# A decoder layer on one core: gate matrices from float32r parts, and differential heads with tokens on partitions

## The chip, the cores and the metric

The kernel runs on one core of a Trainium2 chip. The metric is the device time of one execution in microseconds, as the median over runs. The core has five engines with instruction streams of their own: TensorE (matrix products; PE in the profile, its weight loads PEld), VectorE (DVE), ScalarE (ACT), GpSimd (POOL) and SyncE (SP, which here issues most transfers). Products are accumulated in PSUM, eight banks of 128 partitions x 512 f32; everything else on the chip lies in SBUF.

## The reference, cut to what matters

256 tokens of width 2048 pass one layer. Two token mixers run side by side (latent attention, and differential attention with 8 heads), their gated sum is projected and added to the residual; then comes an expert retrieval over 128 x 128 experts.

A differential head takes the difference of two causal softmaxes, multiplies it with v, and normalizes each token's 128 outputs:

```
p = _causal_probs(q1b, k1, blk, scale) - lam * _causal_probs(q2b, k2, blk, scale)
o = einsum('bhqk,bkhd->bqhd', p, v)
o = rmsnorm(o, g_subln) * (1.0 - lambda_init)
```

The expert retrieval gives each token 8 heads x 16 choices; a choice is a pair (row, col) of keys with a gate, and the expert's number is row * 128 + col:

```
a = gelu(einsum('chkd,cd->chk', expert_u[ec], hc))
w = gc * a
out = einsum('chk,chkd->cd', w, expert_v[ec])
```

## The kernel before, in words

Most weight products are made with float32r operands, a 32-bit type: a weight tile is split into a part `hi` rounded to float32r (ScalarE, L79) and the rest `lo` (VectorE, L84), and both are multiplied (L143 to L145, L161 to L163, L1019). Products on plain f32 operands stand where no split is made, the columns of the expert keys (L721) among them.

**Order of the work.** The program is written in one stream. Helpers with `yield` (a head, a norm) are jobs that `advance` moves on by one part at every eighth product of a block (`tick`), three jobs at a time, so that their short instructions fall between the products. The framework then plans the order of the instructions on each engine from modelled durations and from when tiles and banks come free; each engine works through its own list in that order and waits where something is not ready. `issue_after(x)` keeps an instruction behind x on its own engine. A tile has a tag and a number of buffers; a new tile with that tag waits for the readers of the one that it replaces. PSUM banks are handed out in the same way: `bank(tag)` has one buffer a tag (b0, b1, b2, t, m, n), `ps_s` two (s). `ps_m` is the bank m.

**Differential heads** (L558 to L580). They run as jobs beside the gate projections (L587 to L592). A head makes scores and probabilities (L564, `probs`), transposes the probabilities (L493), copies them (L496), and multiplies with v in `pv` (L503, L504), with v as the stationary operand: the result has the 128 channels on partitions and the 256 tokens along the free axis. ScalarE copies it out of bank m (L573). The sum of squares over channels is then a sum over partitions: ScalarE squares (L205), TensorE multiplies the squares with a column of ones (L216, two products of one column), VectorE scales (L222), GpSimd takes the power -1/2 (L225). The factor of a token must come to all partitions, which two products with the identity do (L231), and VectorE multiplies (L579). `split_scaled` writes both parts for the next projection (L192, L193).

**Expert retrieval.** For 192 of the tokens all experts are worked out densely. 128 columns c of keys follow each other; a column is 16 products of 192 tokens (L721) accumulated in one of four banks (b1, m, n, b0 in turn), and ScalarE writes their Gelu into B, a tile [row, c, token] (L907). The other 64 tokens fetch their own experts by gathers: GpSimd issues them (L862) and VectorE works on the rows (L875, L880). B must be multiplied with each token's gate matrix G[row, col], the sum of gates at that pair. G of a token is the product of two one-hot tiles over its 128 choices: R[choice, row] (GpSimd, L927) and C[choice, col], which carries the gate (VectorE, L928). A step (`g_step`, L932) takes four tokens: four products into one s bank (L937), then VectorE multiplies the columns that are done into B (L947) and copies G into the columns that are not yet done (L949); those are multiplied later by GpSimd (L911) when their Gelu comes (L910). `onehots(t4 + 2)` is called at the head of step t4, with 12 buffers each for R and C. The 48 steps are spread over columns 32 to 119 by a count of products (L729). rowT, colT and gateT hold a token's rows, columns and gates with choices on partitions; `r_tr` (L824) fills them.

After the last column the products with expert_v follow (L1019), with the banks b2, t, m, n and s.

Of the kernel before, what the change touches and what calls it, by code (L numbers as in the profile page):

```python
# [7 lines left out]
F32 = mybir.dt.float32  # L8
F32R = mybir.dt.float32r
U32 = mybir.dt.uint32  # L10
AF = mybir.ActivationFunctionType
ALU = mybir.AluOpType
# [6 lines left out]
EPS = 1e-6  # L19
LAMBDA_INIT = 0.8 - 0.6  # L20
NH = 8
NB = 128
TD = 192
TG = T - TD
NLOW = 64
C0 = 32
NG4 = TD // 4
# [5 lines left out]
def hybrid_peer(tc, a, out):  # L33
    nc = tc.nc
    es = ExitStack()

    def pool(stack, name, bufs=1, side=None, space=None):
        kw = {} if space is None else dict(space=space)
        return stack.enter_context(
            tc.tile_pool(name=name, bufs=bufs, side=side, reuse_waits="tile", **kw))  # L40
# [4 lines left out]
    ident = cst.tile([128, 128], F32, name="ident")  # L45
    iota = cst.tile([128, 128], F32, name="iota")
    ones = cst.tile([128, 1], F32, name="ones")
    nhalf = cst.tile([128, 2], F32, name="nhalf")

    state = {"n": 0, "max": 3, "fill": 0, "b": 0, "g": 0, "c": 0, "f": 0, "s": 0, "w": 0}  # L50
# [120 lines left out]
    wk = pool(ups, "wk")  # L171
    pp = pool(es, "pp", space=PSUM)

    def bank(tag):
        return pp.tile([128, 512], F32, tag=tag, name=tag, bufs=1)
# [5 lines left out]
    def ps_s():  # L181
        return pp.tile([128, 512], F32, tag="s", name="s", bufs=2)

    def ps_m():
        return pp.tile([128, 512], F32, tag="m", name="m", bufs=1)

    def w1(name, tag, bufs=2):
        return wk.tile([128, T], F32, tag=tag, name=name, bufs=bufs)

    def split_scaled(dst, src, g, n=256):  # L190

        nc.scalar.activation(dst[:, 0:n], src, AF.Copy, scale=g)  # L192
        nc.vector.scalar_tensor_tensor(dst[:, n:2 * n], src, g, dst[:, 0:n].bitcast(F32),  # L193
                                       op0=ALU.mult, op1=ALU.subtract)
# [265 lines left out]
    gs = uc.tile([128, 1], F32, name="gs")  # L460
# [7 lines left out]
    def probs(scores, scale, lam=None, prev=None):  # L468

        s = wk.tile([128, 384], F32, tag="sc", name="sc", bufs=3)  # L470
        nc.vector.scalar_tensor_tensor(s, scores[:, 0:384], scale, mask, op0=ALU.mult, op1=ALU.add)
        mx = wk.tile([128, 2], F32, tag="mx", name="mx", bufs=4)
        sm = wk.tile([128, 2], F32, tag="sm", name="sm", bufs=4)
        for tb, c0, c1 in TBK:
            nc.vector.tensor_reduce(mx[:, tb:tb + 1], s[:, c0:c1], axis=AX.X, op=ALU.max, negate=True)
            nc.scalar.activation(s[:, c0:c1], s[:, c0:c1], AF.Exp, bias=mx[:, tb:tb + 1],
                                 accum_out=sm[:, tb:tb + 1])
        rc = wk.tile([128, 2], F32, tag="rc", name="rc", bufs=4)
        nc.vector.reciprocal(rc, sm)
        if lam is not None:  # L480
            nc.vector.tensor_scalar(rc, rc, lam, None, op0=ALU.mult)
        for tb, c0, c1 in TBK:
            if prev is None:
                nc.vector.tensor_scalar(s[:, c0:c1], s[:, c0:c1], rc[:, tb:tb + 1], None, op0=ALU.mult)
            else:
                nc.vector.scalar_tensor_tensor(s[:, c0:c1], s[:, c0:c1], rc[:, tb:tb + 1],
                                               prev[:, c0:c1], op0=ALU.mult, op1=ALU.add)
        return s

    def transposed(s):  # L490
        pt = bank("t")
        for j in range(3):
            nc.tensor.transpose(pt[:, j * 128:(j + 1) * 128], s[:, j * 128:(j + 1) * 128], ident)  # L493

        sT = wk.tile([128, 384], F32, tag="sT", name="sT", bufs=2)
        nc.scalar.activation(sT, pt[:, 0:384], AF.Copy)  # L496
        return sT

    def pv(sT, v, h):

        po = ps_m()
        hs = slice(h * 128, (h + 1) * 128)
        nc.tensor.matmul(po[:, 0:256], lhsT=v[:, 0, hs], rhs=sT[:, 0:256], start=True, stop=False)  # L503
        nc.tensor.matmul(po[:, 128:256], lhsT=v[:, 1, hs], rhs=sT[:, 256:384], start=False, stop=True)  # L504
        return po
# [32 lines left out]
    dv = dfp.tile([128, 2, 1024], F32, name="dv")  # L538
# [5 lines left out]
    for j in range(2):  # L544
        pss = [ps_blk(), ps_blk()]
        group(u_dv, xg, KD, pss)
        for tb in range(2):
            nc.scalar.activation(dv[:, tb, j * 512:(j + 1) * 512], pss[tb], AF.Copy,
                                 scale=r1c[:, tb:tb + 1])
# [5 lines left out]
    oTb = gtp.tile([128, NH, 512], F32R, name="oTb")  # L555
    gt = gtp.tile([128, 32, T], F32, name="gt")

    def diff_head(h):  # L558
        s = None
        for i in range(2):  # L560
            sc = ps_s()
            r0 = i * 64
            for tb, c0, c1 in TBK:
                nc.tensor.matmul(sc[:, c0:c1], lhsT=dq[r0:r0 + 64, h, tb * 128:(tb + 1) * 128],  # L564
                                 rhs=dk[r0:r0 + 64, h, 0:c1 - c0], start=True, stop=True)
            s = probs(sc, 64.0 ** -0.5) if i == 0 else probs(sc, 64.0 ** -0.5, nlam, s)
        yield
        yield
        sT = transposed(s)
        yield  # L570
        po = pv(sT, dv, h)
        on = w1("on", "on", 3)
        nc.scalar.activation(on, po[:, 0:256], AF.Copy)  # L573
        yield
        nm = Norm(1)
        nm.add(on)
        v = nm.col()
        yield
        nc.vector.tensor_mul(on, on, nm.row(v))  # L579
        split_scaled(oTb[:, h], on, gs)  # L580

    for h in range(NH):
        job(diff_head(h))
# [20 lines left out]
    for j in range(KD):  # L604
        m = []
        for u, o, b in ((u_oa, oTa, j), (u_ob, oTb, 16 + j)):
# [4 lines left out]
                                           op0=ALU.add, op1=ALU.mult)  # L611
# [9 lines left out]
    gw = pool(gws, "gw", side="right")  # L621
    rowT = gw.tile([128, 2, 128], F32, name="rowT")
    colT = gw.tile([128, 2, 128], F32, name="colT")
    gateT = gw.tile([128, 2, 128], F32, name="gateT")

    hrep = gw.tile([128, D], F32, name="hrep")
    gidx = gw.tile([128, 64], U32, name="gidx")
# [22 lines left out]
    nm = Norm(KD, nc.gpsimd)  # L650
# [101 lines left out]
    def ps_g():  # L752
        return ps_s().rearrange("p (a b) -> p a b", a=4)
# [11 lines left out]
    for tb in (1, 0):  # L765
# [58 lines left out]
        def r_tr(env=env, tb=tb):  # L824
            pg = ps_g()
            for n, key in enumerate((0, 1, "g")):
                nc.tensor.transpose(pg[:, n, :], env[key].rearrange("p h k -> p (h k)"), ident)
            for n, dst in enumerate((rowT, colT, gateT)):
                nc.vector.tensor_copy(dst[:, tb, :], pg[:, n, :])

        steps.append(r_alloc)
        steps += [lambda b=b, f=r_list: f(b) for b in range(16)]
# [16 lines left out]
        if tb == 1:  # L849
            steps.append(r_list_experts)  # L850
        steps.append(r_tr)


# [43 lines left out]
    def Bsl(c0, c1):  # L897
        if c0 >= NLOW:
            return Bhigh[0][:, c0 - NLOW:c1 - NLOW]
        return Blow[:, c0:c1]  # L900
# [17 lines left out]
    RC = {}  # L918

    def onehots(t4):  # L920
        rc = []
        for i in range(4):
            tb, tt = divmod(4 * t4 + i, 128)
            R = gp.tile([128, 128], F32, tag="R", name="R", bufs=12)
            C = gp.tile([128, 128], F32, tag="C", name="C", bufs=12)
            row, col, gate = [x[:, tb, tt:tt + 1] for x in (rowT, colT, gateT)]
            nc.gpsimd.tensor_scalar(R, iota, row, None, op0=ALU.is_equal)  # L927
            nc.vector.tensor_scalar(C, iota, col, gate, op0=ALU.is_equal, op1=ALU.mult)  # L928
            rc.append((R, C))
        RC[t4] = rc  # L930

    def g_step(t4):  # L932
        if t4 + 2 < NG4:
            onehots(t4 + 2)
        pg = ps_g()
        for i, (R, C) in enumerate(RC.pop(t4)):
            nc.tensor.matmul(pg[:, i, :], lhsT=R, rhs=C, start=True, stop=True)  # L937
        ts_ = slice(4 * t4, 4 * t4 + 4)
        n = state["c"]
        for c0, c1 in sorted({(0, min(n, NLOW)), (NLOW, max(n, NLOW)), (min(n, NLOW), NLOW),  # L940
                              (max(n, NLOW), NB)}):
            if c0 == c1:
                continue
            bv = Bsl(c0, c1)[:, :, ts_].rearrange("p c t -> p t c")
            g = pg[:, :, c0:c1]
            if c0 < n:
                nc.vector.tensor_mul(bv, bv, g)  # L947
            else:
                nc.vector.tensor_copy(bv, g)  # L949
        state["g"] += 1  # L950

    GU0, GU = 14, 80 / 128
# [17 lines left out]
    gps = ExitStack()  # L970
    gp = pool(gps, "gp")
    onehots(0)
    onehots(1)
    fill += [lambda t4=t4: g_step(t4) for t4 in range(NG4)]
    for c in range(C0, NB):
        ps = ps_u()
# [84 lines left out]
    for half in range(2):  # L1061
# [17 lines left out]
        for c in range(NB):  # L1079
            raw = fetch(a["ev"][half, c])  # L1080
            hl = split(raw)
            parts = [[p[:, q * 512:(q + 1) * 512] for p in hl] for q in range(2)]
# [144 lines left out]
```

## Time and profile before

| | us |
|---|---|
| median of 3 runs | 2114.86 (2112.35 to 2115.91) |
| the profiled execution, its own time | 2112.38 |
| its span, first to last instruction | 2110.6 |
| TensorE busy in the span | 2088.1 |
| VectorE busy | 1423.9 |
| ScalarE busy | 791.9 |
| GpSimd busy | 527.0 |

The span is the time between the first and the last instruction of the program; the execution has 1.8 us around it. A busy time is the union of an engine's instructions. The chain that ended last is followed back from the last instruction, at each step to what released it, so its pieces show what a stretch of time was spent on: where TensorE's products follow each other, a piece is what a product adds, while the duration of a single instruction also has the part in which it overlaps its neighbours.

### The profile page before, as it was taken

To read this page: it belongs to the slowest core of one execution; us is meant where nothing else is said; L and a number is where in the kernel's file an instruction comes from. 1 tells how busy PE (TensorE), PEld (TensorE's weight loads), DVE (VectorE), ACT (ScalarE), POOL (GpSimd) and SP (SyncE) were. 2 spreads that over 40 slices of the span, in tenths; PEclk is the share of its full clock that TensorE was granted. 3 is DMA by queue.
4 is the path that set the end of the run, shared out by engine and by line. 5 is a ranking of instruction groups with operands and counts; after the bars stand their busy time and mean duration, and the time that the engine had idled before them with its cause. 6 is when DMAs were issued, how large, how long until landed. Compare 5 with 4: busy or idle time off the path is not lost.

```text
span 2110.6 us, 30529 instructions
## 1 busy us (share of the span) xinstructions
PE 2088.1 (99%) x11446; PEld 1855.9 (88%) x11446; DVE 1423.9 (67%) x2507; ACT 791.9 (38%) x1310; POOL 527.0 (25%) x511
## 2 busy tenths in 40 slices
PE   9999999999999999999999999999999999999998
PEld 7887888888888899999999999999788888888775
DVE  7677667657865988444555555554788888788774
ACT  5545456555554530100000000001455555455554
POOL 0000000000023212335666667662111111112100
PEclk9999999999999999999999999999999999999999
DMA  6563643555566566898888888888888888888774
GB/s 220 180 209 109 201 158 124 190 190 190 190 204 220 166 218 245 295 344 317 316 315 313 319 316 309 310 325 301 320 324 311 322 306 318 310 320 308 300 283 144
DMA packets 132708, 546.78 MB, mean 259 GB/s; under 512 B 15120, under 2 KB 15696, under 8 KB 116048
## 3 DMA queue, kind: packets, MB, share of 16 engines
q1 hardware_dynamic: 112032, 404.60, 54.3%
q0 software_dynamic: 19520, 136.91, 17.4%
q10 hardware_dynamic: 1008, 3.32, 0.4%
q8 instruction: 90, 1.47, 0.3%
q14 instruction: 58, 0.48, 0.1%
HBM read 537.89 MB, written 4.19 MB: 257 GB/s over the span
## 4 chain that ended last, share of the span: by engine, by line
PE 96%; DMA 2%; DVE 1%; issue 0%; ACT 0%; DVEq 0%; POOLq 0%; POOL 0%; ACTq 0%; SPq 0%
PE b L143 19%; PE b L721 16%; PE b L145 10%; PE s L1019 8%; PE n L721 8%; PE m L721 8%; PE m L1019 5%; PE n L1019 5%; PE b L1019 4%; PE t L1019 4%; PE s L937 2%; DMA raw<-in_ev 2%; PE b L161 1%; PE b L163 1%; PE b L162 1%; DVE lo L84 1%
## 5 line engine op out<-in xcount | busy, mean ns | idle before, releaser
L84 DVE TENSOR_TENSOR lo<-raw,hi 128x1024 fp32r<-128x1024 f32 (+1 forms) x504 | 611.9, 1219 | 267.4 <-ACT hi L79 132.5
L79 ACT ACTIVATE hi<-raw 128x1024 fp32r<-128x1024 f32 (+1 forms) x504 | 532.2, 1057 | 527.2 <-PE b L143 131.5
L721 PE MATMUL b<-h,raw 128*128 128x192 f32 x2048 | 342.0, 326 | 0.0
L721 PEld LDWEIGHTS b<-h,raw 128*128 128x128 f32 x2048 | 333.1, 190 | 0.0
L143 PE MATMUL b<-xg,hi 128*128 128x512 f32 x912 | 323.2, 397 | 0.0
L145 PE MATMUL b<-xg,lo 128*128 128x256 f32 x912 | 256.2, 281 | 1.6 <-DVE lo L84 1.6
L143 PEld LDWEIGHTS b<-xg,hi 128*128 128x128 f32 x912 | 171.2, 188 | 42.6 <-issue 4.3
L1019 PE MATMUL s<-hi,wt 128*128 128x512 f32 x512 | 202.9, 397 | 0.0
L145 PEld LDWEIGHTS b<-xg,lo 128*128 128x128 f32 x912 | 171.7, 188 | 2.7 <-DVE lo L84 2.6
L721 PE MATMUL n<-h,raw 128*128 128x192 f32 x1024 | 173.3, 326 | 0.0
L721 PE MATMUL m<-h,raw 128*128 128x192 f32 x1024 | 173.3, 326 | 0.0
L862 POOL DMA_INDIRECT rows<-in_evn,gidx x64 | 91.6, 1430 | 310.2 <-DVE gacc L880 276.3
L721 PEld LDWEIGHTS m<-h,raw 128*128 128x128 f32 x1024 | 166.9, 190 | 0.0
L721 PEld LDWEIGHTS n<-h,raw 128*128 128x128 f32 x1024 | 166.9, 190 | 0.0
L875 DVE SCALAR_TENSOR_TENSOR rows<-rows,hrep 128x2048 f32<-128x2048 f32 x64 | 148.7, 2324 | 14.3 <-DMA rows<-in_eun,gidx 12.9
L880 DVE SCALAR_TENSOR_TENSOR gacc<-rows,gwt,gacc 128x2048 f32<-128x2048 f32 x63 | 148.3, 2354 | 1.2 <-DMA rows<-in_evn,gidx 1.2
L927 POOL TENSOR_SCALAR R<-iota,rowT 128x128 f32<-128x128 f32 x192 | 133.9, 709 | 43.1 <-PE s L937 40.5
L862 POOL DMA_INDIRECT rows<-in_eun,gidx x64 | 76.3, 1192 | 253.2 <-DVE rows L875 193.1
L911 POOL TENSOR_TENSOR Bhigh<-Bhigh,ut 128x192 f32<-128x192 f32 (+28 forms) x64 | 98.9, 1546 | 88.1 <-ACT ut L910 80.5
L1019 PEld LDWEIGHTS s<-hi,wt 128*128 128x128 f32 x512 | 96.0, 188 | 23.9 <-issue 0.5
L1019 PE MATMUL s<-lo,wt 128*128 128x512 f32 x256 | 101.4, 396 | 2.5 <-DVE lo L84 2.5
L928 DVE TENSOR_SCALAR C<-iota,colT,gateT 128x128 f32<-128x128 f32 x192 | 62.8, 379 | 60.6 <-PE s L937 60.2
(322 smaller groups left out, 3444.3 us busy)
## 6 DMA issues: line engine op xcount, KB each, us to landing
raw<-in_eu SPq DMA_DIRECT2D x256, 512.0 KB
raw<-in_ev SPq DMA_DIRECT2D x256, 512.0 KB
raw<-in_w_in SPq DMA_DIRECT2D x133, 512.0 KB
raw<-in_w_out SPq DMA_DIRECT2D x32, 512.0 KB
raw<-in_w_q SPq DMA_DIRECT2D x32, 512.0 KB
raw<-in_w_o_mla SPq DMA_DIRECT2D x16, 512.0 KB
raw<-in_w_o_diff SPq DMA_DIRECT2D x16, 512.0 KB
raw<-in_w_uq SPq DMA_DIRECT2D x9, 512.0 KB
```

The costliest lines, as they stand in the source:

```text
L79: state["hi"] = nc.scalar.activation(hi[:, c], raw[:, c], AF.Copy).ins
L84: state["lo"] = nc.vector.tensor_sub(lo[:, c], raw[:, c], hi[:, c].bitcast(F32)).ins
L143: nc.tensor.matmul(ps[0:m, 0:512], lhsT=hi, rhs=act[:, k, :], start=(k == 0), stop=False)
L145: state["mm"] = nc.tensor.matmul(ps[0:m, 0:256], lhsT=lo, rhs=act[:, k, 0:256], start=False, stop=(k == nk - 1)).ins
L721: mm = nc.tensor.matmul(ps[:, 0:TD], lhsT=u_raw[-1][:, k % 8 * 128:(k % 8 + 1) * 128], rhs=h2[:, k], start=(k == 0), stop=(k == KD - 1), s ...
L862: nc.gpsimd.indirect_dma_start(out=g, out_offset=None, in_=a["eun" if which == "u" else "evn"], in_offset=bass.IndirectOffsetOnAxis(ap=gid ...
L875: nc.vector.scalar_tensor_tensor(g, g, 1.0, hrep, op0=ALU.mult, op1=ALU.mult, accum_out=gdot[:, j:j + 1])
L880: nc.vector.scalar_tensor_tensor(gacc, g, gwt[:, j:j + 1], gacc, op0=ALU.mult, op1=ALU.add)
L911: nc.gpsimd.tensor_mul(b[:, 0:n], b[:, 0:n], t[:, 0:n])
L927: nc.gpsimd.tensor_scalar(R, iota, row, None, op0=ALU.is_equal)
L928: nc.vector.tensor_scalar(C, iota, col, gate, op0=ALU.is_equal, op1=ALU.mult)
L1019: nc.tensor.matmul(o, lhsT=l, rhs=r, start=first and i == 0, stop=last and i == len(ops) - 1, skip_group_check=True)
```

## The change

A head's product with v takes the transposed probabilities as the stationary operand, so tokens come to lie on partitions: three products of 128 columns. The sum of squares of a token is then a sum along the free axis, which ScalarE accumulates while it squares (one instruction for each half of the tokens), and the factor is a scalar of each partition, applied by VectorE straight from bank m. Two transposes into bank n bring the result back to channels on partitions, and `split_scaled` reads them from there.

The gate of a token is kept as a rounded float32r part gh, its negative ng, and the rest gl. R is float32r; C has 256 columns, the one-hot with gh in the first half, made by ScalarE as Relu(gh - gh * Abs(col - iota)), and the one-hot with gl in the second, made by VectorE. One product for each token gives both halves of G. They are added as they leave the banks: ScalarE copies the second half out, VectorE adds the first where B is multiplied at once, and otherwise adds both into B. A step has two halves of two tokens, each in a bank of its own (b2 and t, or the two s). `onehots` runs one step ahead in place of two, with 8 buffers in place of 12.

```diff
--- before.py
+++ after.py
@@ -568,16 +568,32 @@
         yield
         sT = transposed(s)
         yield
-        po = pv(sT, dv, h)
+
+        po = ps_m()
+        hs = slice(h * 128, (h + 1) * 128)
+        for tb, parts in ((0, ((0, 0),)), (1, ((1, 0), (2, 1)))):
+            for i, (c, kb) in enumerate(parts):
+                nc.tensor.matmul(po[:, tb * 128:(tb + 1) * 128], lhsT=sT[:, c * 128:(c + 1) * 128],
+                                 rhs=dv[:, kb, hs], start=(i == 0), stop=(i == len(parts) - 1),
+                                 skip_group_check=True)
         on = w1("on", "on", 3)
-        nc.scalar.activation(on, po[:, 0:256], AF.Copy)
-        yield
-        nm = Norm(1)
-        nm.add(on)
-        v = nm.col()
-        yield
-        nc.vector.tensor_mul(on, on, nm.row(v))
-        split_scaled(oTb[:, h], on, gs)
+        ss = wk.tile([128, 2], F32, tag="nv", name="nv", bufs=4)
+        for tb in range(2):
+            cs = slice(tb * 128, (tb + 1) * 128)
+            nc.scalar.activation(on[:, cs], po[:, cs], AF.Square, accum_out=ss[:, tb:tb + 1])
+        nc.vector.tensor_scalar(ss, ss, 1.0 / 128, EPS, op0=ALU.mult, op1=ALU.add)
+        r = wk.tile([128, 2], F32, tag="nr", name="nr", bufs=4)
+        nc.gpsimd.tensor_tensor(r, ss, nhalf, op=ALU.pow)
+        for tb in range(2):
+            cs = slice(tb * 128, (tb + 1) * 128)
+            nc.vector.tensor_scalar(on[:, cs], po[:, cs], r[:, tb:tb + 1], None, op0=ALU.mult)
+        yield
+        yield
+        pt = bank("n")
+        for tb in range(2):
+            cs = slice(tb * 128, (tb + 1) * 128)
+            nc.tensor.transpose(pt[:, cs], on[:, cs], ident)
+        split_scaled(oTb[:, h], pt[:, 0:256], gs)
 
     for h in range(NH):
         job(diff_head(h))
@@ -621,7 +637,10 @@
     gw = pool(gws, "gw", side="right")
     rowT = gw.tile([128, 2, 128], F32, name="rowT")
     colT = gw.tile([128, 2, 128], F32, name="colT")
-    gateT = gw.tile([128, 2, 128], F32, name="gateT")
+
+    ghT = gw.tile([128, 2, 128], F32R, name="ghT")
+    ngT = gw.tile([128, 2, 128], F32, name="ngT")
+    glT = gw.tile([128, 2, 128], F32, name="glT")
 
     hrep = gw.tile([128, D], F32, name="hrep")
     gidx = gw.tile([128, 64], U32, name="gidx")
@@ -825,8 +844,11 @@
             pg = ps_g()
             for n, key in enumerate((0, 1, "g")):
                 nc.tensor.transpose(pg[:, n, :], env[key].rearrange("p h k -> p (h k)"), ident)
-            for n, dst in enumerate((rowT, colT, gateT)):
+            for n, dst in enumerate((rowT, colT)):
                 nc.vector.tensor_copy(dst[:, tb, :], pg[:, n, :])
+            nc.scalar.activation(ghT[:, tb, :], pg[:, 2, :], AF.Copy)
+            nc.scalar.activation(ngT[:, tb, :], ghT[:, tb, :].bitcast(F32), AF.Copy, scale=-1.0)
+            nc.vector.tensor_sub(glT[:, tb, :], pg[:, 2, :], ghT[:, tb, :].bitcast(F32))
 
         steps.append(r_alloc)
         steps += [lambda b=b, f=r_list: f(b) for b in range(16)]
@@ -921,32 +943,43 @@
         rc = []
         for i in range(4):
             tb, tt = divmod(4 * t4 + i, 128)
-            R = gp.tile([128, 128], F32, tag="R", name="R", bufs=12)
-            C = gp.tile([128, 128], F32, tag="C", name="C", bufs=12)
-            row, col, gate = [x[:, tb, tt:tt + 1] for x in (rowT, colT, gateT)]
+            R = gp.tile([128, 128], F32R, tag="R", name="R", bufs=8)
+            C = gp.tile([128, 256], F32R, tag="C", name="C", bufs=8)
+            A = gp.tile([128, 128], F32, tag="A", name="A", bufs=2)
+            row, col, gh, ng, gl = [x[:, tb, tt:tt + 1] for x in
+                                    (rowT, colT, ghT.bitcast(F32), ngT, glT)]
             nc.gpsimd.tensor_scalar(R, iota, row, None, op0=ALU.is_equal)
-            nc.vector.tensor_scalar(C, iota, col, gate, op0=ALU.is_equal, op1=ALU.mult)
+            nc.scalar.activation(A, iota, AF.Abs, bias=col, scale=-1.0)
+            nc.scalar.activation(C[:, 0:128], A, AF.Relu, bias=gh, scale=ng)
+            nc.vector.tensor_scalar(C[:, 128:256], iota, col, gl, op0=ALU.is_equal, op1=ALU.mult)
             rc.append((R, C))
         RC[t4] = rc
 
     def g_step(t4):
-        if t4 + 2 < NG4:
-            onehots(t4 + 2)
-        pg = ps_g()
-        for i, (R, C) in enumerate(RC.pop(t4)):
-            nc.tensor.matmul(pg[:, i, :], lhsT=R, rhs=C, start=True, stop=True)
-        ts_ = slice(4 * t4, 4 * t4 + 4)
-        n = state["c"]
-        for c0, c1 in sorted({(0, min(n, NLOW)), (NLOW, max(n, NLOW)), (min(n, NLOW), NLOW),
-                              (max(n, NLOW), NB)}):
-            if c0 == c1:
-                continue
-            bv = Bsl(c0, c1)[:, :, ts_].rearrange("p c t -> p t c")
-            g = pg[:, :, c0:c1]
-            if c0 < n:
-                nc.vector.tensor_mul(bv, bv, g)
-            else:
-                nc.vector.tensor_copy(bv, g)
+        if t4 + 1 < NG4:
+            onehots(t4 + 1)
+        rc = RC.pop(t4)
+        for h in range(2):
+            pg = (ps_s() if t4 % 2 else bank(("b2", "t")[h])).rearrange("p (a b c) -> p a b c", a=2, b=2)
+            for i in range(2):
+                R, C = rc[2 * h + i]
+                nc.tensor.matmul(pg[:, i], lhsT=R, rhs=C, start=True, stop=True)
+
+            gl = gp.tile([128, 2, 128], F32, tag="gl", name="gl", bufs=2)
+            nc.scalar.activation(gl, pg[:, :, 1, :], AF.Copy)
+            ts_ = slice(4 * t4 + 2 * h, 4 * t4 + 2 * h + 2)
+            n = state["c"]
+            if n:
+                nc.vector.tensor_add(gl[:, :, 0:n], gl[:, :, 0:n], pg[:, :, 0, 0:n])
+            for c0, c1 in sorted({(0, min(n, NLOW)), (NLOW, max(n, NLOW)), (min(n, NLOW), NLOW),
+                                  (max(n, NLOW), NB)}):
+                if c0 == c1:
+                    continue
+                bv = Bsl(c0, c1)[:, :, ts_].rearrange("p c t -> p t c")
+                if c0 < n:
+                    nc.vector.tensor_mul(bv, bv, gl[:, :, c0:c1])
+                else:
+                    nc.vector.tensor_add(bv, gl[:, :, c0:c1], pg[:, :, 0, c0:c1])
         state["g"] += 1
 
     GU0, GU = 14, 80 / 128
@@ -970,7 +1003,6 @@
     gps = ExitStack()
     gp = pool(gps, "gp")
     onehots(0)
-    onehots(1)
     fill += [lambda t4=t4: g_step(t4) for t4 in range(NG4)]
     for c in range(C0, NB):
         ps = ps_u()
```

## Rows read from the trace of the kernel before

**Rows 1.** The page, busy time of each engine in the whole span.
```profile
PE 2088.1 (99%) x11446; PEld 1855.9 (88%) x11446; DVE 1423.9 (67%) x2507; ACT 791.9 (38%) x1310; POOL 527.0 (25%) x511
```
**Rows 2.** The page, chain that ended last, shares of the span by line.
```profile
PE b L143 19%; PE b L721 16%; PE b L145 10%; PE s L1019 8%; PE n L721 8%; PE m L721 8%; PE m L1019 5%; PE n L1019 5%; PE b L1019 4%; PE t L1019 4%; PE s L937 2%; DMA raw<-in_ev 2%; PE b L161 1%; PE b L163 1%; PE b L162 1%; DVE lo L84 1%
```
**Rows 3.** Busy us in two stretches, then granted clock, DMA share, GB/s.
```profile
285.00:370.00 85.00, 84.93 (x518) 71.46 (x517) 65.43 (x167) 56.72 (x138) 6.66 (x8) 1.00 0.39 130
945.00:1440.00 495.00, 495.00 (x3168) 495.00 (x3167) 256.54 (x498) 34.47 (x175) 317.55 (x329) 1.00 0.87 315
```
**Rows 4.** Waits of TensorE, the longest total: us, times, longest one.
```profile
PE s L270 <- ACT wz L268: 2.7, 1, 2.7
```
**Rows 5.** Chain, 1302 to 1304 us: start, what it adds, line and count.
```profile
1302.76 0.89 PE s L937 x8
```
**Rows 6.** Groups of TensorE by shape: busy us, mean ns, idle before.
```profile
L145 PE MATMUL b<-xg,lo 128*128 128x256 f32 x912 | 256.2, 281 | 1.6 <-DVE lo L84 1.6
...
L937 PE MATMUL s<-C,R 128*128 128x128 f32 x384 | 50.6, 275 | 0.0
```
**Rows 7.** Chain in a block of float32r products, 399.9 to 401.3 us.
```profile
399.87 0.23 PE b L143
400.10 0.12 PE b L145
```
**Rows 8.** Lines 937 and 927: ns least/median/most, first and last start.
```profile
L937 PEld LDWEIGHTS s<-C,R x384: 190/192/192, 948.0 to 1438.7; 128*128 128x128 f32 x192
...
L927 POOL TENSOR_SCALAR R<-iota,rowT x192: 590/602/2737, 907.9 to 1410.3; 128x128 f32<-128x128 f32 x192
```
**Rows 9.** Chain in the heads' stretch, 350.2 to 354 us.
```profile
350.80 0.25 PE t L493 x2
...
352.44 0.34 PE n L216 x4
352.78 0.54 PE m L503 x2
353.32 0.22 PE m L504 x2
```
**Rows 10.** The same view, 308.8 to 310.4 us.
```profile
309.60 0.44 PE n L231 x4
310.04 0.43 PE m L503 x2
```
**Rows 11.** Lines 592 and 150 on ScalarE: ns least/median/most, first and last start.
```profile
L592 ACT ACTIVATE gt<-z,bh x32: 492/510/512, 299.3 to 493.3; 128x256 f32<-128x256 f32 x32
...
L150 ACT ACTIVATE z<-b x32: 361/364/385, 293.9 to 492.0; 128x256 f32<-128x256 f32 x32
```
**Rows 12.** Groups of VectorE by shape, 945 to 1440 us.
```profile
L947 DVE TENSOR_TENSOR Blow<-Blow,s 128x256 f32<-128x256 f32 x30 | 21.3, 711 | 2.5 <-PE s L937 2.5
```
**Rows 13.** SyncE's queue, longest wait of the column loads: us, times, longest.
```profile
SPq L70 <- PE b L721: 276.5, 116, 3.1
```
**Rows 14.** Timeline of TensorE, 300.9 to 310.2 us: start, us, line.
```profile
301.17 0.60 PE L503 MATMUL m<-sT,dv 128*128 128x256 f32 x2
...
305.56 0.68 PE L503 MATMUL m<-sT,dv 128*128 128x256 f32 x2
```
**Rows 15.** Timeline of ScalarE, 302 to 311.5 us.
```profile
306.90 0.37 ACT L573 ACTIVATE on<-m 128x256 f32<-128x256 f32 x1
```
**Rows 16.** Groups by shape in the heads' stretch, 285 to 370 us.
```profile
L84 DVE TENSOR_TENSOR lo<-raw,hi 128x1024 fp32r<-128x1024 f32 x21 | 25.7, 1223 | 16.8 <-PE b L145 8.9 <-issue 6.3 <-PE b L162 1.6
...
L225 POOL TENSOR_TENSOR nr<-nv,nhalf 128x2 f32<-128x2 f32 x8 | 6.7, 832 | 106.6 <-DVE nv L222 106.6
...
L476 ACT ACTIVATION_READ_ACCUMULATOR sc<-sc,mx 128x1 f32 x32 | 6.0, 188 | 0.0
...
L484 DVE TENSOR_SCALAR sc<-sc,rc 128x128 f32<-128x128 f32 x8 | 2.2, 281 | 0.0
```
**Rows 17.** Line 907 on ScalarE, its table loads.
```profile
L907 ACT ACT_TABLE_LOAD  x3: 1283/1283/1283, 777.2 to 847.8; - x3
```

## The prediction

> **What bounds the kernel now.** I read the busy times first: TensorE is busy 2088.1 of 2110.6 us [rows 1]. A busy matmul row is no proof, so next the chain that ended last, by line: nearly all of it is matmul lines, the gate matrices' own (L937) with 2% [rows 2]. The table of stretches then says the same of both places that the change touches: in 945 to 1440, where the gate matrices are made, TensorE is busy 495.00 of 495 us at a granted clock of 1.00 (2.4 GHz), in 285 to 370, where the differential heads run, 84.93 of 85; VectorE has 256.54, ScalarE 34.47 and GpSimd 317.55 of the 495 [rows 3]. Last the waits of TensorE: the longest total is 2.7 us, at the very start [rows 4]. So a microsecond of matmul taken out of either stretch is a microsecond of the span, as long as the other engines stay ahead, and work added to them is free until one falls behind.
>
> **Gate matrices, TensorE.** A step makes four tokens' matrices and there are 48 steps. Now a step takes 0.89 us of the chain, in 8 matmuls [rows 5]: 384 matmuls for 192 tokens, so an f32 product is two passes, while the 912 products of the float32r line L145, 256 columns each, are 912 matmuls, one pass each [rows 6]. Among its neighbours such a 256-column pass adds 0.12 us to the chain [rows 7]. The new product is of that shape and type, four a step: 0.48 us. Gain 48 x (0.89 - 0.48) = 19.7 us. What I can't see is four of them in a row, each behind its own weight load, which takes 190 ns from start to end [rows 8]. From above, if nothing of the load were hidden: 4 x 0.19 = 0.76 us a step, gain 6.2 us; from below, 0.11 us, today's pass (0.89 / 8), gain 21.6. I take 0.12, the same shape and type; today's passes of 0.11 us hide loads just as long.
>
> **Differential heads, TensorE.** Removed per head: the sum over ones, 0.34 us [rows 9], the row broadcast, 0.44, and the product with v, 0.43 [rows 10] and 0.22 [rows 9]; together 1.43 us. Added: three 128 x 128 products in two passes each at 0.11 (half of that 0.22), 0.66, and two transposes, 0.25 [rows 9]; together 0.91. Gain 8 x 0.52 = 4.2 us; bounds 3.3 and 5.0, since the product with v also appears with 0.54 in place of 0.43 [rows 9], and such 0.11 us a head can fall to the old form or the new.
> Here the Trainium skill speaks against the change: "TensorE: Matmul & The Clock Gate", section "Part 4: PE-mode transpose", gives about 275 ns for a transpose among other work. By that figure the 16 transposes would cost an estimated 4.4 us where the rows make it 2.0, and the time would come out 2.4 us later. The trace has the 275 ns too, as the duration of one; what the chain pays is less, since neighbours overlap it.
>
> **What is added beside TensorE, and its cover.** The step period is (1438.7 - 948.0) / 47 = 10.44 us [rows 8], after the change 10.03.
> ScalarE had 34.47 / 495 x 10.44 = 0.73 us a step. It gets eight 128-column activations with pointer operands, at most 0.51 us each (a 256-column one with a bias), 4.1, and two copies of 256 columns out of PSUM at 0.37, 0.7 [rows 11]: 5.6 us of 10.03.
> VectorE had 5.4 us. The one-hot C stays one instruction a token. An addition per half comes new, at most 0.71 each (its nearest row is the multiply of 256 elements [rows 12]), and the multiplies and copies of 512 elements a step, 1.4 by that row, are cut in halves, which at most doubles them: 8.2 of 10.03.
> GpSimd keeps its four R a step and 6.7 us. Its results become float32r; no row has GpSimd writing that, ScalarE and VectorE do at their usual pace, so I take nothing, with a doubling of R's 0.60 us [rows 8] (9.1 us a step, still under the period) as the bad end and no gain as the good one, since R's time hides anyway.
> The one-hots lose distance: with 12 buffers the last R began at 1410.3, 28 us before its matmul [rows 8]; with 8 they run one period less ahead, some 18 us. That is the cover for everything queued before them: on GpSimd's queue the row gathers (an R that waits for a buffer holds the next gather behind it, as today), on ScalarE the Gelu evacuations, which free TensorE's ring of four banks and so have three columns of (10.44 - 0.89) / 1.83 = 5.2 us (a step follows 1.83 columns), 15 us. If ScalarE waited on a C buffer it would be for the step before last, which TensorE has always passed by then. The product banks (b2, t and the two s) come round every second step.
> The transfers move nowhere, but the stretch asks for the same bytes in 20 us less: the DMA share goes from 0.87 to about 0.91. SyncE's loads wait for TensorE to free a buffer, 276.5 us in the first such row [rows 13], not TensorE for loads; there is distance left.
> In r_tr a copy becomes two activations and a subtraction, twice in the kernel, under a column loop: nothing.
>
> **The heads' new wait.** The single bank m used to come free when ScalarE had copied it; now it is held through squares, scale, power and the second multiply. Products with v follow each other at 4.39 us [rows 14], in runs of three, three and two: five follow closely. Chain: ScalarE reaches m 1.34 us after the product starts [rows 14, 15]; two squares with their accumulator reads at most 2 x (0.51 + 0.19), 1.4; the power 0.83; three small VectorE instructions at most 0.28 each, 0.84 [rows 16]: 4.4 us, about the gap. Two queueings behind a lo of 1.22 us each [rows 16] add 0 to 2.4, so five heads cost 0 to 12 us. I take 0: the order of the instructions is planned ahead from when a bank is due, and today's bank n is handed on in the same way with no TensorE wait on the list [rows 4]. Queued behind that product on TensorE would be everything.
>
> **Sum.** 19.7 + 4.2 = 23.9 us off the profiled execution's 2112.38 gives 2088.5. The median of the three runs, 2114.86, is 2.5 above that execution, so the forecast for the median is **2091.0**. The measurement can tell about 0.2%, 4.2 us, from no change.
>
> **Rivals.**
> (a) Bank m is waited for in full: 2103. For it speaks a chain as long as the gap, against it the clean list of waits. Chance 0.10.
> (b) The 256-column products run at the pace of their loads, 0.19: gain 10.4, 2104.5. Against it, neighbours of 0.11 with the same loads. Chance 0.05.
> (c) The change doesn't do what it says: the products stay two passes. A 256-column f32 pass takes 0.215 us (half of 0.43 [rows 10]), a step 1.72: 48 x 0.83 = 39.8 more, less 4.2, 2150.5. Against it, one matmul per product in L145's count. Chance 0.03.
> (d) The other side, as one mechanism: table loads on ScalarE. Abs and Relu come between Gelus; a load takes 1283 ns [rows 17]. ScalarE's 5.6 us a step reach the period of 10.03 from four loads a step on. One before each of the eight activations is 10.3 us: 15.9 a step, 48 x 5.9 = 283 us later, 2374. Against it, three loads in all at the evacuations of before, though only Gelu and Exp meet there, so the trace does not settle it. Chance 0.02.
> On (d) the Trainium skill, "ScalarE: Activation LUTs", section "Table sets: the hidden batching unit", says that cheap functions such as relu and abs are in every set as filler. By that rule no load comes with them; no run so far shows it, and it keeps the chance of (d) low.
>
> **Numbers.** Forecast 0.78, (a) 0.10, (b) 0.05, (c) 0.03, (d) 0.02; 0.02 for shifts in the planned order that eat all of it. The range goes from 2084 (the good ends of both stretches, 2.7 us; 2.5 for runs as low as the lowest shown, 2112.35; 2 for shifts in the planned order) to 2104 (all of (a), and (b) at its edge). Faster by over 0.2%: 0.93; within: 0.02; slower: 0.05.
>
> **What would show it.** Right: the gate-matrix line with 192 matmuls at about 0.12 us each of the chain, a step 0.48; the stretch of columns shorter by some 20 us and still full; the sum over ones and the row broadcast gone; no TensorE wait longer than 1 us at the head's product. Wrong: 384 matmuls there (c); 0.19 each (b); waits at the product with v for VectorE (a); table loads by the hundred on ScalarE and TensorE waiting for C (d); or a list of TensorE waits that grew where nothing was changed.

## The result and the profile after

The changed kernel takes 2092.3 us, the median of four runs (2088.43 to 2094.27); the kernel before, beside them, 2115.3 (median of four). The ratio is 0.9894, with a 95% interval of 0.9879 to 0.9908: 1.1% faster. The forecast was 2091.0.

The profiled execution took 2090.91 us, 21.5 less than that of before. By stretches: the columns of keys, from the first to the last product, take 20.2 us less, what lies ahead of them 1.4 less, what follows them the same within 0.2. The column products in bank b before (nanoseconds least, median and most, first and last start); the same line of the changed kernel stands further down:

```profile
L721 PE MATMUL b<-h,raw x2048: 326/326/328, 770.9 to 1480.4; 128*128 128x192 f32 x187
```

The page of the changed kernel, busy time and the chain by line:

```profile
PE 2063.1 (99%) x11222; PEld 1830.1 (88%) x11222; DVE 1459.0 (70%) x2754; ACT 947.4 (45%) x1810; POOL 504.2 (24%) x511
...
PE b L143 18%; PE b L740 16%; PE b L145 9%; PE s L1051 8%; PE n L740 8%; PE m L740 8%; PE n L1051 5%; PE m L1051 5%; PE b L1051 4%; PE t L1051 4%; DMA raw<-in_ev 1%; DVE lo L84 1%; PE b L162 1%; PE b L161 1%; PE b L163 1%
```

TensorE lost 25.0 us of busy time and is still the bound; the gate-matrix line, 2% in [rows 2], has left the list. The two stretches in the changed kernel (busy us of PE, PEld, DVE, ACT and POOL, clock, DMA share, GB/s):

```profile
285.00:358.00 73.00, 70.16 (x437) 57.77 (x436) 62.44 (x169) 50.26 (x148) 6.34 (x8) 1.00 0.39 131
945.00:1420.00 475.00, 475.00 (x2977) 475.00 (x2977) 289.75 (x738) 185.57 (x637) 307.42 (x333) 1.00 0.90 328
```

Against [rows 3], the stretch of columns is as full as it was. ScalarE went from 34.47 to 185.57 us and TensorE waits for it nowhere in the stretch; VectorE does, 7.4 us for the copies out of the banks, and has room for it. The heads' stretch is no longer full: 2.8 us of TensorE are idle.

A step of the gate matrices in the chain (start, us added, line), against [rows 5]:

```profile
1196.99 0.47 PE s L966 x4
```

The lines that answer to [rows 8], the R instruction and half of the weight loads, with the Relu that writes C and the column products in bank b:

```profile
L966 PEld LDWEIGHTS s<-C,R x96: 187/190/193, 956.5 to 1417.1; 128*128 128x128 f32 x96
...
L951 POOL TENSOR_SCALAR R<-iota,rowT x192: 590/603/2463, 906.5 to 1399.5; 128x128 fp32r<-128x128 f32 x192
...
L953 ACT ACTIVATE C<-A,ghT,ngT x192: 477/490/514, 907.7 to 1399.7; 128x128 fp32r<-128x128 f32 x192
...
L740 PE MATMUL b<-h,raw x2048: 323/326/328, 769.5 to 1458.8; 128*128 128x192 f32 x187
```

The whole gain of the stretch is in the first fence of these two: four passes of 0.12 us in place of eight of 0.11, 0.42 us a step and 20.2 us in 48 steps. The last R begins at 1399.5, 18 us before its matmul at 1417. Writing float32r costs GpSimd nothing (a median of 603 ns, 602 before).

Where the waits grew: TensorE's waits in the heads' stretch, 285 to 360 us (us, times, longest), and VectorE's for GpSimd there. The kernel before has none of either in 285 to 370 us.

```profile
PE t L493 <- DVE sc L486: 1.9, 3, 1.3
PE m L576 <- DVE on L589: 0.8, 1, 0.8
...
DVE on L589 <- POOL nr L586: 4.4, 8, 0.9
```

### The profile page after: what moved, and what is told of

Its sections match the earlier page's. It is cut to its first block, busy times and chain, and to the rows that moved or that the text cites. A ratio compares the mean times of both kernels' runs of the same rounds, so it can differ in the third digit from the quotient of the medians.

```text
span 2089.2 us, 31015 instructions
## 1 busy us (share of the span) xinstructions
PE 2063.1 (99%) x11222; PEld 1830.1 (88%) x11222; DVE 1459.0 (70%) x2754; ACT 947.4 (45%) x1810; POOL 504.2 (24%) x511
## 4 chain that ended last, share of the span: by engine, by line
PE 93%; DMA 3%; DVE 3%; ACT 1%; issue 1%; POOL 0%; DVEq 0%; POOLq 0%; ACTq 0%; SPq 0%
PE b L143 18%; PE b L740 16%; PE b L145 9%; PE s L1051 8%; PE n L740 8%; PE m L740 8%; PE n L1051 5%; PE m L1051 5%; PE b L1051 4%; PE t L1051 4%; DMA raw<-in_ev 1%; DVE lo L84 1%; PE b L162 1%; PE b L161 1%; PE b L163 1%
## 5 line engine op out<-in xcount | busy, mean ns | idle before, releaser
L143 PE MATMUL b<-xg,hi 128*128 128x512 f32 x912 | 325.6, 399 | 0.3 <-DVE xg L251 0.2
L143 PEld LDWEIGHTS b<-xg,hi 128*128 128x128 f32 x912 | 171.2, 188 | 44.7 <-issue 3.6
L884 POOL DMA_INDIRECT rows<-in_evn,gidx x64 | 83.9, 1310 | 316.5 <-DVE gacc L902 273.4
L951 POOL TENSOR_SCALAR R<-iota,rowT 128x128 fp32r<-128x128 f32 x192 | 128.3, 680 | 40.2 <-PE s L966 21.4
L953 ACT ACTIVATE C<-A,ghT,ngT 128x128 fp32r<-128x128 f32 x192 | 89.2, 491 | 98.3 <-PE b L966 57.4
L954 DVE TENSOR_SCALAR C<-iota,colT,glT 128x128 fp32r<-128x128 f32 x192 | 62.1, 372 | 63.4 <-PE s L966 36.4
L933 POOL TENSOR_TENSOR Bhigh<-Bhigh,ut 128x192 f32<-128x192 f32 (+28 forms) x64 | 86.8, 1358 | 70.2 <-ACT ut L932 62.9
```

The source lines that it names most:

```text
L143: nc.tensor.matmul(ps[0:m, 0:512], lhsT=hi, rhs=act[:, k, :], start=(k == 0), stop=False)
L884: nc.gpsimd.indirect_dma_start(out=g, out_offset=None, in_=a["eun" if which == "u" else "evn"], in_offset=bass.IndirectOffsetOnAxis(ap=gid ...
L933: nc.gpsimd.tensor_mul(b[:, 0:n], b[:, 0:n], t[:, 0:n])
L953: nc.scalar.activation(C[:, 0:128], A, AF.Relu, bias=gh, scale=ng)
```

## The experiments

**The two parts alone.** gates_only takes the changed kernel and puts the old head back; heads_only is the kernel before with the new head. heads_only, as the edit of before:

```diff
-        po = pv(sT, dv, h)
+        po = ps_m()
...
-        nc.vector.tensor_mul(on, on, nm.row(v))
-        split_scaled(oTb[:, h], on, gs)
+        split_scaled(oTb[:, h], pt[:, 0:256], gs)
```

> The gate matrices from float32r parts alone, the heads as before. Theory (TensorE is the bound, one pass per 256-column product): a step takes 0.47 us of the chain instead of 0.89, the stretch of columns gets 48 x 0.42 = 20.1 us shorter, everything ahead of it is as before; about 2095.2 us, ratio 0.9905. Rival (the two parts of the change help each other, by the order of the instructions that is planned anew): the gain is not 20 but some 17 or 23 us. On the pace of the gate projections (16 pairs of products in 5.55 us before, in 5.66 after): if the planned order up to there sets it, 5.55 here, for the order up to there is that of before; if each execution draws it anew, either.

Measured: 0.9904 (0.9891 to 0.9918), 2094.1 us. Its column products in bank b:

```profile
L724 PE MATMUL b<-h,raw x2048: 323/326/328, 774.1 to 1463.3; 128*128 128x192 f32 x187
```

First to last it is 689.2 us, the 689.3 of the changed kernel. The gain of the gate matrices stands by itself.

> The heads with tokens on partitions alone, the gate matrices as before. Theory: 4.2 us of products go, some 2 us come back as waits of the transposes of the next head's probabilities, since VectorE waits for GpSimd's power with them behind it; the products of the gate projections then run at 5.66 us per 16 pairs instead of 5.55, which takes some 2.5 us more: in all 0.5 to 1.5 us faster, ratio 0.9993 to 0.9998, not to be told from the kernel before. If the pace is drawn anew in each execution and is not a matter of the heads: 3.4 us faster, 0.9984. Rival (heads cost nothing, the sum of the prediction holds): 4.2 us faster, 0.998, no waits at L493.

Measured: 0.9984 (0.9975 to 0.9993), 2110.18 us, so 3.4 us faster. The first and last tanh of the 32 gate projections beside which the heads run:

```profile
L607 ACT ACTIVATE gt<-z,bh x32: 493/509/512, 298.8 to 491.9; 128x256 f32<-128x256 f32 x32
```

That is 193.1 us. [rows 11] have 194.0 for the profiled execution of before, 0.9 us more and not 3.4. The next two runs bear on that.

**The same kernels again.** No edit; the changed kernel and the kernel before.

> The changed kernel once more, for the spread and the pace of the gate projections. If the pace is a matter of the planned order: 5.66 us per 16 pairs again, the heads' gain lost over 358 to 490 us again, 2091 us. If it is drawn in each execution: 5.55 is as likely, and then the profiled time is some 2.5 us lower, 2088.5.

> The kernel before, once more, as the measure of no change: ratio 1.0000 with an interval of about 0.0015 to either side. Pace of the gate projections 5.55 us per 16 pairs again if the planned order sets it, 5.55 or 5.66 if it is drawn in each execution.

Measured: 0.9901 (0.9886 to 0.9916) and 1.0002 (0.9988 to 1.0016). The tanh line of the changed kernel again, then of the kernel before again:

```profile
L608 ACT ACTIVATE gt<-z,bh x32: 493/509/512, 300.0 to 493.2; 128x256 f32<-128x256 f32 x32
```

```profile
L592 ACT ACTIVATE gt<-z,bh x32: 498/511/513, 300.5 to 497.1; 128x256 f32<-128x256 f32 x32
```

The same program of before took 194.0 us in one execution and 196.6 in another. In the first one, the second pair of products after the one that begins at 399.87 in [rows 7] begins at:

```profile
400.56 0.23 PE b L143
```

The chain in the second one:

```profile
399.81 0.23 PE b L143
400.04 0.12 PE b L145
400.16 0.24 PE b L143
400.40 0.12 PE b L145
400.52 0.23 PE b L143
```

Two pairs take 0.71 us where the first execution took 0.69: every second pair is 14 ns longer by the starts of the matmuls, at a granted clock of 1.00 in both. Over the gate projections after the heads, 384 pairs, this is 135.7 us against 133.2. Of the twelve profiled executions of all kernels here, eleven have 135.7 in that place, gates_only with the old heads among them, and only the first one of before 133.2. So my reading that the heads slowed these products fell: the same program shows both paces, so the pace is not a matter of the change, and 2.5 us of the gain were hidden by it in the first pair of profiles. What sets it stays open; the runs don't separate the execution from the chip that it ran on. Against 196.6 the heads are worth 3.5 us, which is what heads_only was timed at.

**What a pass costs.** g_f32 makes R and C plain f32; g_128 multiplies with the first half of C alone.

```diff
-            R = gp.tile([128, 128], F32R, tag="R", name="R", bufs=8)
-            C = gp.tile([128, 256], F32R, tag="C", name="C", bufs=8)
+            R = gp.tile([128, 128], F32, tag="R", name="R", bufs=8)
+            C = gp.tile([128, 256], F32, tag="C", name="C", bufs=8)
```

> R and C as plain f32 in place of float32r, all else as changed: the 256-column product in two passes. Theory (the gain is the passes saved): 8 matmuls a step of about 0.215 us each, a step 1.72 us, 48 x (1.72 - 0.47) = 60 us slower than the changed kernel, about 2152 us, 38 us slower than before. Rival (the gain came with the order of the steps or the banks): within 20 us of the changed kernel.

Measured: 2150.43 us in one run. The chain at a step:

```profile
1207.52 1.73 PE s L966 x8
```

The column products in bank b:

```profile
L740 PE MATMUL b<-h,raw x2048: 326/326/328, 771.3 to 1520.8; 128*128 128x192 f32 x187
```

A step of 1.73 us and 60.2 us more from first to last product: the time goes with the passes, and with the same steps, banks and one-hots the change in f32 would have been some 37 us slower than before (2113.3 beside it).

```diff
-                nc.tensor.matmul(pg[:, i], lhsT=R, rhs=C, start=True, stop=True)
+                nc.tensor.matmul(pg[:, i, 0], lhsT=R, rhs=C[:, 0:128], start=True, stop=True)
...
-            nc.scalar.activation(gl, pg[:, :, 1, :], AF.Copy)
+            nc.scalar.activation(gl, pg[:, :, 0, :], AF.Copy, scale=0.0)
```

> The product of float32r parts with the first 128 columns alone; the part with the gates' rests, gl, is left out of the sum. It shows what a pass of half the columns costs. If a pass costs by its columns: 0.06 us, a step 0.24, 48 x 0.23 = 11 us faster than changed. If the load behind it is what is left (f32 passes of 128 columns stand at 0.11): 0.11 each, a step 0.44, 1 to 2 us faster. If float32r needs 256 columns for its pace: 0.21 each, a step 0.86, 19 us slower.

Measured: 2088.24 us in one run. The chain at a step:

```profile
1196.68 0.40 PE s L966 x4
```

The column products in bank b:

```profile
L740 PE MATMUL b<-h,raw x2048: 326/326/378, 769.9 to 1457.9; 128*128 128x192 f32 x187
```

By this piece a pass would cost 0.10 us. But from the first to the last product all 48 steps save only 1.3 us, 0.027 each, so a step costs 0.44 and a pass 0.11. The rest shows behind the step, where 60 column products take 0.05 us more than in the changed kernel (its line first):

```profile
997.23 9.75 PE b L740 x60
```

```profile
997.37 9.80 PE b L740 x60
```

Half the columns thus save 6% of the step: most of what a pass of 128 float32r columns costs does not go with its columns. The second expectation, 0.44 a step and 1 to 2 us faster, is the one that came true. That the load behind it is what is left is not shown by this. The second half of C, which carries the gates' rests, is almost free.

**Is the work beside TensorE covered?** Every Abs and Relu of the one-hots is issued twice.

```diff
             nc.scalar.activation(A, iota, AF.Abs, bias=col, scale=-1.0)
+            nc.scalar.activation(A, iota, AF.Abs, bias=col, scale=-1.0)
+            nc.scalar.activation(C[:, 0:128], A, AF.Relu, bias=gh, scale=ng)
             nc.scalar.activation(C[:, 0:128], A, AF.Relu, bias=gh, scale=ng)
```

> Each Abs and each Relu of the one-hots is done twice: ScalarE's work in the stretch of columns grows by 48 x 4 x 0.7 = 134 us, from 186 to about 320 of 475. Theory (work beside TensorE is covered while its engine has room in the period and runs ahead): no change, within 2 us of the changed kernel, and no TensorE wait at the gate-matrix line. Rival (the one-hots are near their limit with one step ahead): TensorE waits for C at every step, 48 x 1 us or more.

Measured: 2088.29 us in one run, at the lower edge of the runs of the changed kernel (2088.43 to 2095.74). From the first to the last product it is 689.2 us, as without the edit. The stretch of columns:

```profile
945.00:1420.00 475.00, 475.00 (x2978) 475.00 (x2977) 289.69 (x736) 311.06 (x1003) 308.30 (x333) 1.00 0.90 328
```

ScalarE rose by 125 us and TensorE is still busy all 475. The cover holds with much to spare.

**The heads' missing part.** mult_late lets ScalarE copy the result out of bank m, takes the squares and multiplies from that copy, and puts VectorE's multiplies one part of the job later.

```diff
+        sq = w1("sa", "sa")
...
+        nc.scalar.activation(on, po[:, 0:256], AF.Copy)
...
-            nc.scalar.activation(on[:, cs], po[:, cs], AF.Square, accum_out=ss[:, tb:tb + 1])
+            nc.scalar.activation(sq[:, cs], on[:, cs], AF.Square, accum_out=ss[:, tb:tb + 1])
...
-            nc.vector.tensor_scalar(on[:, cs], po[:, cs], r[:, tb:tb + 1], None, op0=ALU.mult)
-        yield
+        yield
+        with tc.issue_after(state["lo"]):
+            for tb in range(2):
+                cs = slice(tb * 128, (tb + 1) * 128)
+                nc.vector.tensor_scalar(on[:, cs], on[:, cs], r[:, tb:tb + 1], None, op0=ALU.mult)
         yield
```

> The changed kernel, with the head's result copied out of bank m by ScalarE as before the change, and VectorE's two multiplies by the factor put one part of the job later (behind a lo), so that GpSimd's power is done when VectorE comes to them. Theory (the heads' missing 2 to 3 us are VectorE standing before the multiplies for GpSimd's power, with the next head's probabilities behind them, and bank m held): TensorE's waits at L493 (1.9 us) and at the product with v (0.8) go, from the start of the gate projections to the end of the heads TensorE needs some 6 us less than before the change instead of 3.4; about 2090.0 us, 0.9889 of before. Rival (the waits come from elsewhere on VectorE, which is full there): 1.9 us at L493 stays, within 0.5 us of the changed kernel in that stretch.

Measured: 0.9867 (0.9846 to 0.9887), 2086.78 us, the lowest median of all. Its interval still touches that of the changed kernel, so what the edit is worth is read from the traces. The tanh line:

```profile
L611 ACT ACTIVATE gt<-z,bh x32: 492/509/511, 298.7 to 489.2; 128x256 f32<-128x256 f32 x32
```

TensorE's waits in the heads' stretch, and VectorE's for GpSimd:

```profile
PE m L576 <- ACT sT L496: 0.4, 2, 0.2
...
DVE on L593 <- POOL nr L588: 4.3, 6, 0.9
```

190.5 us against 196.6: 6.1 less than before, 2.6 less than the change, as expected. Both waits of TensorE are gone; a new one of 0.4 us, for the copy of the transposed probabilities (L496), has come. But VectorE stands for GpSimd nearly as long as it did, 4.3 us for 4.4. What that is worth the halves ask.

copy_only has the copy and the squares of mult_late and multiplies at once; late_only multiplies later, straight from bank m.

```diff
 copy_only
-            nc.vector.tensor_scalar(on[:, cs], po[:, cs], r[:, tb:tb + 1], None, op0=ALU.mult)
+            nc.vector.tensor_scalar(on[:, cs], on[:, cs], r[:, tb:tb + 1], None, op0=ALU.mult)
 late_only
+        yield
+        with tc.issue_after(state["lo"]):
+            for tb in range(2):
...
```

> One half of mult_late: ScalarE copies the head's result out of bank m, VectorE multiplies at once, before the job's next part, so it still stands for GpSimd's power. Theory (two waits, one by bank m, one by VectorE standing): the wait at the product with v, 0.8 us, goes, the 1.9 us at the transposes L493 stay; the heads' stretch, 66.97 us in the changed kernel and 64.32 in mult_late, takes 66.2. Rival (the copy does it all): 64.3. Rival (the place of the multiplies does it all): 67.

> The other half of mult_late: the multiplies one part later, but straight from bank m, which is held until then. Theory: the 1.9 us at L493 go, and bank m is held a part longer, so the next product with v comes late: waits at it of 1 us or more, or the planned order moves it back among the other products at no cost; 64.5 to 66.5 us for the heads' stretch. Rival (the place does nothing): 67.

Measured, in one run each: 2093.74 us for copy_only and 2093.14 for late_only. One run can't rank them beside the changed kernel (2088.43 to 2095.74), so the traces are read. By the starts of the matmuls L143, number 544 to 672, the heads' stretch takes 70.4 us before, 66.97 changed, 65.58 in copy_only, 66.71 in late_only and 64.32 in mult_late. TensorE's waits there, copy_only and then late_only:

```profile
PE m L576 <- ACT sT L496: 1.1, 2, 0.9
PE n L597 <- DVE oTb L193: 0.3, 1, 0.3
```

```profile
PE t L493 <- DVE sc L486: 1.3, 1, 1.3
PE b L145 <- DVE lo L84: 0.9, 1, 0.9
PE m L576 <- DVE on L591: 0.4, 2, 0.2
```

Both miss their expectation. copy_only lost the wait at L493, which I had put down to VectorE standing; late_only, where nothing of the next head should stand behind the multiplies, kept 1.3 us of it. So the simple story, one wait for each half, fell. VectorE at the place of that wait, late_only and then copy_only (start, us, and in brackets the idle time before with its releaser):

```profile
307.19 0.35 DVE L591 TENSOR_SCALAR on<-m,nr 128x128 f32<-128x128 f32 x1 [0.69 <-POOL nr L586]
307.46 0.74 DVE L486 SCALAR_TENSOR_TENSOR sc<-sc,rc 128x128 f32<-128x128 f32 x2
```

```profile
307.05 0.75 DVE L486 SCALAR_TENSOR_TENSOR sc<-sc,rc 128x128 f32<-128x128 f32 x2
...
308.70 0.48 DVE L591 TENSOR_SCALAR on<-on,nr 128x128 f32<-128x128 f32 x2 [0.50 <-POOL nr L588]
```

In late_only the multiply still stands ahead of the next head's probabilities (L486): in the planned order the edit did not move it there. In copy_only it comes behind them, and VectorE's standing for GpSimd costs TensorE nothing at that place. So this wait goes with which of the two comes first. Shown is also that the two edits together take 2.65 us, the copy alone 1.4 and the place alone 0.3. Why the planned order turns with one edit and not with the other was not settled.

## Why the prediction was right, point by point

**Gate matrices.** The term was 19.7 us, by 0.48 a step; measured 0.47 and 20.2. The shape and type of the neighbours' row was the right price. Rival (b), the pace of the loads, is out: a pass of 0.12 us here and of 0.11 in g_128 is well under the 0.19 of a load. Rival (c) did not happen, and its price, a step of 1.72, was met by g_f32 with 1.73. Rival (d) is out: there are as many loads as in [rows 17],

```profile
L929 ACT ACT_TABLE_LOAD  x3: 1283/1283/1283, 775.8 to 846.5; - x3
```

and none at the new activations. By the rule of the Trainium skill, "ScalarE: Activation LUTs", section "Table sets: the hidden batching unit", cheap functions come with every set; the trace agrees for Abs and Relu beside Gelu. The bounds on the other engines held: 3.9 us a step on ScalarE (5.6 allowed), 6.1 on VectorE (8.2), 6.5 on GpSimd; DMA share 0.90 (0.91).

**Heads.** The term was 4.2 us, measured 3.4, and it came near by luck. The products themselves save more: nearly without waits, in mult_late, 6.1 us. The two new groups cost what was said, in the chain of the changed kernel:

```profile
310.19 0.22 PE n L595 x2
310.41 0.67 PE m L576 x6
```

That is 0.89 a head against the 0.91 forecast; so the side of before was sized too low. The 1.43 us were taken from one clean place each. Counted from the start of each matmul to the next, idle time left out, over the heads' stretch (L143 number 544 to 672), the removed products took 12.6 us before, 1.58 a head, and the new ones take 7.0. That is 5.6 us, above the prediction's bound of 5.0. Another 1.5 us come from the scores (L564), which the change does not edit and the prediction does not count: 7.8 us before, 6.3 in the newly planned order. The gate projections and the other transposes take 0.9 more, and TensorE's idle 2.8 us leave the 3.4.
The 275 ns for a transpose from "TensorE: Matmul & The Clock Gate" of the Trainium skill, section "Part 4: PE-mode transpose", would have made the pair an estimated 0.55; the chain shows 0.22.

**The new wait** is the step that failed. I took 0 for it and followed bank m alone, where it is 0.8 us. The 1.9 us at L493 were not on my list: I had not asked what stands behind the multiply on VectorE, which waits for GpSimd there. The prediction named this as a sign of being wrong, a list of TensorE waits that grew where nothing was changed: the transposes at L493 were not edited. Of the 1.9 us 1.26 fall at one place, in the changed kernel around 306 us, on VectorE, GpSimd and TensorE:

```profile
305.34 0.35 DVE L589 TENSOR_SCALAR on<-m,nr 128x128 f32<-128x128 f32 x1 [0.69 <-POOL nr L586]
305.61 0.74 DVE L486 SCALAR_TENSOR_TENSOR sc<-sc,rc 128x128 f32<-128x128 f32 x2
...
304.60 0.70 POOL L586 TENSOR_TENSOR nr<-nv,nhalf 128x2 f32<-128x2 f32 x1 [58.38 <-ACT z L150]
...
306.10 0.30 PE L493 MATMUL t<-ident,sc 128*128 128x128 f32 x1 [1.26 <-DVE sc L486]
```

A power of 0.70 us held the multiply, the next head's probabilities (L486) came after it, and TensorE's transposes after those. Around 330 us it is the same with a power of 1.50 us, and TensorE stands for 0.4. Rival (a) was of this kind, at another place and a fifth of its price. Two errors of 2 to 3 us, the products' gain too small and the waits left out, nearly cancelled.

**The sum.** 23.9 us were forecast. gates_only and heads_only have 0.0096 and 0.0016, together 1.1%, 24 us, and the change itself 0.0106; within their intervals the parts add up. By the traces it is 20.2 and 3.4, 23.6 us.

## What to carry to other kernels

Where TensorE is the bound, count passes: an f32 product of 128 columns is two passes of 0.11 us, and the same product from float32r parts, twice as wide, is one of 0.12. The work that was moved beside TensorE for this cost nothing here, since its engines had room in the period and ran a step ahead; doubling it, as on ScalarE, is a cheap way to see that. Check a piece of the chain against the whole stretch: the step of 0.40 us in g_128 was worth 0.44. When a value now comes from a slow engine to a full one, ask not only who waits for the result but what stands behind the instruction that waits.

## What the runs showed of the hardware

The pace of float32r pairs has two values in the same program at a granted clock of 1.00: by the starts of the matmuls 0.347 us for every pair, or 0.346 and 0.361 in turn, and it stays at either for a hundred us and more. For the gate projections after the heads this is 133.2 or 135.7 us, and it differed between two executions of the kernel before. What sets it stays open. A comparison of two single profiles over 190 us can thus be off by 2.5 us with nothing changed.

A float32r pass of 128 columns costs 0.11 us by the steps of g_128, one of 256 columns 0.12.
